# Moving the sample stream's attention beside the gate projections, applying the attention gate at the output projection's input, and spacing the probability split two blocks behind the scores

## The chip, the cores and the metric

The kernel runs on one core of a Trainium2 chip. The metric is the time of one execution in microseconds (us) on the device. The kernel before takes 1334.92 us, the median of three runs between 1334.04 and 1336.14 us.

## The reference

One layer of a streaming encoder for 1024 new frames of one stream (the prompt) and 32 new frames of a running stream (the sample), D = 1024, 16 heads of 64. The two streams differ only in their history: the sample attends to 512 cached frames as well, and its convolution continues a saved state.

```python
h = rmsnorm(x, norm_g)                       # then every projection of h, 1024 columns each:
q = rmsnorm(cols(OFF_Q, ...)) * HEAD_DIM ** -0.5;  k = rmsnorm(cols(OFF_K, ...));  v = cols(OFF_V, ...)
logf = log_sigmoid(cols(OFF_F, N_HEADS) + b_f)
ga, gb, ma, mb = ...                         # gates
u = cols(OFF_UA, ...) * sigmoid(cols(OFF_UB, ...))
s = einsum('bqhd,bkhd->bhqk', q, k) + C[t] - C[s]          # C = cumsum(logf), causal mask
o = softmax(s) @ v
ya = (o * silu(ga)) @ w_pa
yb = (silu(layernorm(causal_dwconv(u))) * silu(gb)) @ w_pb
y = x + (sigmoid(ma) * ya + sigmoid(mb) * yb) @ w_out
```

The results are y, k, v, logf and the convolution's last 30 rows, for both streams.

## The kernel before

**Layout.** Channels lie on the 128 partitions in eight tiles, frames along the free axis: 1056 columns (1024 prompt frames and 32 sample frames), worked in three pieces of 352. A projection of 128 output channels is 24 steps ("beats"): for each of three pieces, eight steps of three matmuls, because every operand is kept as a high and a low part (xh, xl, wh, wl) and three of the four products are formed.

**Stages in order of time**, with the stretches of the profiled execution: the first projections, the convolution's input and v (to about 184 us); k and q (184 to 496), where line 969 makes the high halves `qh` and line 970 the low halves `ql`, which go to DRAM; the projection of the gate `ga` (496 to 579); the prompt's attention (579 to 1036); the remainder of the gate projections and the loads for the next stage (1036 to 1064); the three output projections pa, pb and out (to the end).

**What sets the order.** In the first stages TensorE, VectorE and ScalarE run in the order in which the code issues their instructions; the other queues are ordered by the compiler's scheduler. `beat()` (line 204) counts steps, lets `prep` and `late` jobs out when their step has come, and hands out convolution taps (line 379 on VectorE) from the list `taps` at a rate per step. `begin()` (line 226) plans the next pair of weights: load at steps 5 and 15, sum of squares on ScalarE, a total by a small matmul, then the split into `wh` and `wl`. In the attention stage SyncE, which issues the DMAs, also runs in written order, and an instruction that waits holds up those behind it.

**The prompt's attention.** There are eight groups of two heads. Each group has 16 blocks ("units"): eight query blocks of 128 frames for each of two heads, with 128 to 1024 keys. A unit goes through `scores` (TensorE, into one of two PSUM tiles `psS`), `top` (VectorE, the row maximum), `soft` (ScalarE, the exponential P, which frees `psS`), `factor` (VectorE, the reciprocal of the sum), `high` (ScalarE, P times the factor as 16-bit values in PH), `low` (the rest of P into PH's second half: VectorE for the first head, two GpSimd instructions for the second), and `turn` (SyncE, a transposing DMA from PH to PT). In round k the loop issues unit k's scores and then `factor` and `high` of unit k-1, so `high` of one unit stands on ScalarE ahead of `soft` of the next. Between them `fill_for` issues steps of the projections gb, ma and mb, in proportion to the unit's width plus 320; they keep TensorE busy. P and PH have three buffers each. `values(m)` multiplies the turned halves with v for two query blocks, LAG = 5 rounds behind, and `gated(m)` scales the result (ScalarE) and multiplies it by the gate's slice (GpSimd, line 1282), which `load_gate` (line 1258) fetched; the product goes to DRAM as `s_o`.

**The sample's attention** (`class Sample`, lines 1114 to 1193) handles four heads at a time: loads of cached keys and values and of the cumulative forget sums, scores, maximum, exponential, normalization, five transposes, the product with the values, and one more transpose. Its four parts are put into groups 1, 2, 4 and 6 of the prompt's attention (`SAT`), and take their PSUM tiles from the two pools that the prompt's units use (`psS` and `psT`, two tiles each).

**After the attention.** `a_half(f)` (line 1426) loads a tile of `s_o`, adds the sample's columns, and splits it into `ah` (ScalarE) and `al` (VectorE). Its tiles come from the pool `bg` with five buffers, which the layer norm's output `ln_out` (line 1435) shares. There TensorE alone runs in written order: the last two gate projections, then pa, whose first tile takes its eight input tiles f = 0 to 7 in turn, three pieces of three matmuls each.

Of the kernel before, what the change touches and what calls it, by code (L numbers as in the profile page):

```python
# [18 lines left out]
T = 1024  # L19
TS = 32  # L20
# [17 lines left out]
LAG = 5  # L38
# [4 lines left out]
SAT = (1, 2, 4, 6)  # L43
# [14 lines left out]
def build(tc, xT, xt, wv, wf, ckT, cv, clT, stT, vec, cst, yT, kT, vO, lfO, cpT, csT):  # L58
# [167 lines left out]
    def begin():  # L226
# [21 lines left out]
        if after:  # L248
            jobs += [(5 + 10 * i, after.load) for i in range(after.n)]
# [679 lines left out]
    def qk(g, f):  # L929
# [96 lines left out]
    def gate_steps(g, f, pj):  # L1026
        def ev(c, sl, ps, inv):
            t = t352("t", 3)
            if g == "ga":
                sides["silu"] = nc.scalar.activation(t, ps, AF.Silu, scale=inv)  # L1030
            else:
                nc.scalar.mul(t, ps, inv)
            stored(lambda: nc.sync.dma_start(s_g[g][f, :, sl], t))

        return steps((g, f), X, XL, pj, ev)
# [37 lines left out]
    tables_again("silu")  # L1073
# [3 lines left out]
    order.close()  # L1077
    pcv.close()
# [35 lines left out]
    class Sample:  # L1114


        def __init__(self, g):
            self.g = g

        def load(self):  # L1120
            g = self.g
            self.kc = kc = ap.tile([128, 2, PAST], F32, name="kc", tag="kc", bufs=1)
            nc.sync.dma_start(kc, ckT[2 * g:2 * g + 2].rearrange("a p n -> p a n"))
            self.vc = vc = ap.tile([128, 4, 256], F32, name="vc", tag="vc", bufs=1)
            nc.sync.dma_start(vc, cv[:, :, 256 * g:256 * g + 256])
            self.pf = pf = ap.tile([128, SKEYS], F32, name="pf", tag="pf", bufs=1)
            for j in range(4):
                nc.sync.dma_start(pf[32 * j:32 * j + 32, :], s_cs[4 * g + j:4 * g + j + 1, :].broadcast_to([32, SKEYS]))

        def scores(self):  # L1130
            g, kc, pf = self.g, self.kc, self.pf
            ps = psS.tile([128, 2, 512], F32, name="psS", tag="S")
            for j in range(4):
                rows = slice(64 * (j % 2), 64 * (j % 2) + 64)
                q = qs_t[rows, 2 * g + j // 2, :]
                nc.tensor.matmul(ps[32 * j:32 * j + 32, 0, :], q, kc[rows, j // 2, :], start=True, stop=True)
                nc.tensor.matmul(ps[32 * j:32 * j + 32, 1, :TS], q, ks_t[rows, 2 * g + j // 2, :],
                                 start=True, stop=True)
            self.ps = ps

        def top(self):
            g, ps, pf = self.g, self.ps, self.pf
            nc.vector.scalar_tensor_tensor(pf[:, :PAST], ps[:, 0, :], cq[:, g:g + 1], pf[:, :PAST],
                                           op0=ALU.add, op1=ALU.subtract)
            nc.vector.scalar_tensor_tensor(pf[:, PAST:], ps[:, 1, :TS], cq[:, g:g + 1], pf[:, PAST:],
                                           op0=ALU.add, op1=ALU.subtract)
            nc.vector.tensor_add(pf[:, PAST:], pf[:, PAST:], smask)
            self.nm = nm = ap.tile([128, 3], F32, name="nmr", tag="nmr", bufs=2)
            nc.vector.tensor_reduce(nm[:, 0:1], pf, axis=AX.X, op=ALU.max, negate=True)

        def soft(self):
            nc.scalar.activation(self.pf, self.pf, AF.Exp, bias=self.nm[:, 0:1], accum_out=self.nm[:, 1:2])

        def norm(self):
            nm, pf = self.nm, self.pf
            nc.vector.reciprocal(nm[:, 2:3], nm[:, 1:2])
            nc.vector.tensor_scalar(pf, pf, nm[:, 2:3], None, op0=ALU.mult)

        def turn(self):
            pf = self.pf  # L1160
            self.pts = pts = ap.tile([128, 7, 128], F32, name="pts", tag="kc", bufs=1)
            g = self.g
            nc.gpsimd.memset(pts[:, 4:7, :], 0.0)
            self.vn = pts[:, 5:7, :].rearrange("p a n -> p (a n)")
            nc.sync.dma_start(pts[:TS, 5:7, :], s_vs[:, 256 * g:256 * g + 256].rearrange("p (a n) -> p a n", a=2))
            pt = psT.tile([128, 512], F32, name="ptr2", tag="T")
            for b in range(4):
                nc.tensor.transpose(pt[:, 128 * b:128 * b + 128], pf[:, 128 * b:128 * b + 128], ident)
            nc.scalar.copy(pts[:, 0:4, :], pt.rearrange("p (b q) -> p b q", b=4))
            pt = psT.tile([128, 512], F32, name="ptr2", tag="T")  # L1170
            nc.tensor.transpose(pt[:TS, :128], pf[:, PAST:], ident)
            nc.scalar.copy(pts[:TS, 4, :], pt[:TS, :128])

        def values(self):

            vc, vn, pts = self.vc, self.vn, self.pts
            po = psT.tile([128, 512], F32, name="po", tag="T")
            for b in range(5):
                for j in range(4):
                    hs = slice(64 * j, 64 * j + 64)  # L1180
                    nc.tensor.matmul(po[32 * j:32 * j + 32, :64], pts[:, b, 32 * j:32 * j + 32],
                                     vc[:, b, hs] if b < 4 else vn[:, hs], start=(b == 0), stop=(b == 4))
            self.oq = ap.tile([128, 64], F32, name="oq", tag="oq", bufs=1)
            nc.scalar.copy(self.oq, po[:, :64])

        def finish(self):

            g = self.g
            pt = psT.tile([128, 512], F32, name="ptr2", tag="T")
            nc.tensor.transpose(pt[:64, :128], self.oq, ident)  # L1190
            p4 = pt[:64, :128].rearrange("d (a b n) -> d a b n", a=2, b=2)
            nc.scalar.copy(os_t[0:64, 2 * g:2 * g + 2, :], p4[:, :, 0, :])
            nc.vector.tensor_copy(os_t[64:128, 2 * g:2 * g + 2, :], p4[:, :, 1, :])

    class Unit:
# [22 lines left out]
        def soft(self):  # L1218
            self.P = ap.tile([128, T], F32, name="P", tag="P", bufs=3)
            with tc.issue_after(sides["tables"].ins):  # L1220
                nc.scalar.activation(self.P[:, :self.w], self.ps[:, :self.w], AF.Exp, bias=self.nm[:, 0:1],  # L1221
                                     accum_out=self.nm[:, 1:2])
# [29 lines left out]
    class Pair2:  # L1252
# [539 lines left out]
```

## Time and profile before

The times are microseconds of one profiled execution, whose span is 1332.6 and whose own time was 1334.77, against the median of 1334.92 of the runs that were timed. "Busy" is the time in which an engine worked; matmuls are pipelined, so their durations overlap, and a busy TensorE is not at its peak. The clock is the share of full speed that TensorE was granted.

| stretch | length | TensorE busy | VectorE busy | ScalarE busy | GpSimd busy | clock | DMA share |
|---|---|---|---|---|---|---|---|
| 0 to 496 (up to k and q) | 496.00 | 481.05 | 418.92 | 314.07 | 263.98 | 0.99 | 0.39 |
| 496 to 579 (gate ga) | 83.00 | 83.00 | 76.46 | 32.96 | 14.35 | 1.00 | 0.39 |
| 579 to 1036 (attention) | 457.00 | 396.35 | 334.85 | 276.35 | 218.09 | 0.95 | 0.88 |
| 1036 to 1070 (last gates, loads) | 34.00 | 34.00 | 17.04 | 23.14 | 11.49 | 1.00 | 0.96 |
| 1070 to the end | 263.00 | 259.36 | 155.28 | 88.26 | 138.52 | 1.00 | 0.51 |

A row of such a view has the stretch, its length, and for each engine the busy time and the number of instructions in brackets, then the granted clock, the mean busy share of the 16 DMA engines (it can come out above 1) and what they moved in GB/s. In a row of waits stand the instruction that waited, what released it, the sum of the waits, their number and the longest.

### The profile page before, as it was taken

To read this page: it belongs to the slowest core of one execution; us is meant where nothing else is said; L and a number is where in the kernel's file an instruction comes from. 1 tells how busy PE (TensorE), PEld (TensorE's weight loads), DVE (VectorE), ACT (ScalarE), POOL (GpSimd) and SP (SyncE) were. 2 spreads that over 40 slices of the span, in tenths; PEclk is the share of its full clock that TensorE was granted. 3 is DMA by queue.
4 is the path that set the end of the run, shared out by engine and by line. 5 is a ranking of instruction groups with operands and counts; after the bars stand their busy time and mean duration, and the time that the engine had idled before them with its cause. 6 is when DMAs were issued, how large, how long until landed. Compare 5 with 4: busy or idle time off the path is not lost. (4 is left out here: it accounts for less than half of the span.)

```text
span 1332.6 us, 24984 instructions
## 1 busy us (share of the span) xinstructions
PE 1253.8 (94%) x9270; PEld 928.6 (70%) x9270; DVE 1002.5 (75%) x1494; ACT 734.8 (55%) x1376; POOL 646.4 (49%) x622
## 2 busy tenths in 40 slices
PE   8999999998999899998888797988899999999999
PEld 5687876665666566665555564655566699999998
DVE  6799899796988889889787786776566485166674
ACT  5555555766685763456465465756666565133320
POOL 4067674636474632125473454435445286155562
PEclk9999999999999999999899897999999999999999
DMA  6244342424233354349889799989988887444362
GB/s 255 99 123 123 84 121 67 121 77 125 88 112 114 88 167 135 133 120 200 220 173 219 157 211 221 203 174 223 241 193 173 317 270 250 138 130 143 124 214 69
DMA packets 270554, 213.66 MB, mean 160 GB/s; under 512 B 188001, under 2 KB 232929, under 8 KB 270433
## 3 DMA queue, kind: packets, MB, share of 16 engines
q1 hardware_dynamic: 270288, 212.01, 59.3%
q8 instruction: 72, 1.18, 0.4%
q14 instruction: 50, 0.40, 0.1%
q10 hardware_dynamic: 144, 0.07, 0.0%
HBM read 115.04 MB, written 59.22 MB: 131 GB/s over the span
## 5 line engine op out<-in xcount | busy, mean ns | idle before, releaser
L188 PE MATMUL pj<-xh,wh 128*128 128x352 f16 (+2 forms) x1536 | 487.1, 317 | 6.6 <-DVE qn L959 6.3
L188 PE MATMUL pj<-xl,wh 128*128 128x352 f16 (+2 forms) x1536 | 486.2, 317 | 1.4 <-DVE xl L599 1.3
L188 PE MATMUL pj<-xh,wl 128*128 128x352 f16 (+2 forms) x1536 | 486.4, 317 | 0.1
L188 PEld LDWEIGHTS <-wh 128*128 128x128 f16 x3072 | 303.7, 99 | 167.8 <-issue 2.8
L379 DVE SCALAR_TENSOR_TENSOR y<-u,vec_t,y 128x1086 f32<-128x1086 f32 x240 | 356.9, 1488 | 6.2 <-ACT y L376 3.1
L188 PEld LDWEIGHTS <-wl 128*128 128x128 f16 x1536 | 151.8, 99 | 76.8 <-issue 8.1
L1233 ACT ACTIVATE PH<-P,nm 128x256 f16<-128x256 f32 (+7 forms) x128 | 99.0, 773 | 123.0 <-issue 43.0
L146 DVE SCALAR_TENSOR_TENSOR wl<-raw,sc,wh 128x384 f16<-128x384 f32 x188 | 137.6, 752 | 22.3 <-ACT wh L143 20.9
L1239 POOL TENSOR_SCALAR P<-P,nm 128x128 f32<-128x128 f32 (+3 forms) x64 | 56.6, 885 | 162.5 <-ACT PH L1233 162.1
L1221 ACT ACTIVATE P<-psS,nm 128x256 f32<-128x256 f32 (+7 forms) x128 | 93.6, 731 | 42.0 <-DVE nm L1216 39.4
L1210 PE MATMUL psS<-KB,QB 128*128 128x512 f16 (+2 forms) x192 | 64.2, 334 | 43.3 <-ACT P L1221 43.1
L1216 DVE TENSOR_REDUCE nm<-psS 128x1 f32<-128x256 f32 (+7 forms) x128 | 95.9, 749 | 8.3 <-PE psS L1212 8.2
L180 POOL TENSOR_TENSOR wl<-raw,wh 128x384 fp32r<-128x384 f32 (+1 forms) x51 | 62.8, 1260 | 71.6 <-ACT wh L177 42.9
L1240 POOL TENSOR_TENSOR PH<-P,PH 128x128 f16<-128x128 f32 (+3 forms) x64 | 85.1, 1330 | 5.1
L1242 DVE SCALAR_TENSOR_TENSOR PH<-P,nm,PH 128x128 f16<-128x128 f32 (+3 forms) x64 | 69.0, 1078 | 22.0 <-ACT PH L1233 20.2
L944 POOL TENSOR_TENSOR sql<-sqf,sqh 128x352 fp32r<-128x352 f32 x48 | 54.1, 1127 | 62.8 <-ACT sqh L941 62.6
L970 POOL TENSOR_TENSOR ql<-qn,qh 128x352 f16<-128x352 f32 (+1 forms) x48 | 60.5, 1270 | 20.0 <-ACT qh L969 19.5
L813 PE MATMUL pjv<-vwh,xh 128*128 128x260 f16 x256 | 70.2, 274 | 0.0
L813 PE MATMUL pjv<-vwl,xh 128*128 128x260 f16 x256 | 70.0, 274 | 0.0
L813 PE MATMUL pjv<-vwh,xl 128*128 128x260 f16 x256 | 70.0, 273 | 0.0
L1226 DVE RECIPROCAL nm<-nm 128x1 f32<-128x1 f32 x128 | 20.3, 158 | 61.5 <-ACT P L1221 61.0
L119 ACT ACTIVATE junk<-raw 128x1024 bf16<-128x1024 f32 x62 | 65.0, 1048 | 0.0
(299 smaller groups left out, 2679.9 us busy)
## 6 DMA issues: line engine op xcount, KB each, us to landing
raw<-wf SPq DMA_DIRECT2D x92, 512.0 KB
kT<-kun SPq DMA_DIRECT2D x8, 528.0 KB
s_ga<-t SPq DMA_DIRECT2D x24, 176.0 KB
s_gb<-t SPq DMA_DIRECT2D x24, 176.0 KB
s_ma<-t SPq DMA_DIRECT2D x24, 176.0 KB
s_mb<-t SPq DMA_DIRECT2D x24, 176.0 KB
sma<-s_ma SPq DMA_DIRECT2D x24, 176.0 KB
y<-s_y SPq DMA_DIRECT2D x8, 528.0 KB
```

Of the source, the lines that this page charges most:

```text
L119: nc.scalar.activation(junk[:, :raw.shape[1] * raw.shape[2]], raw.rearrange("p a b -> p (a b)"), AF.Square, accum_out=self.tops[:, i:i + 1])
L146: nc.vector.scalar_tensor_tensor(wl[:, ks, :], raw[:, ks, :], self.s[:, i:i + 1], wh[:, ks, :], op0=ALU.mult, op1=ALU.subtract)
L180: nc.gpsimd.tensor_sub(wl[:, k0:k1, :], raw[:, k0:k1, :], f32(wh[:, k0:k1, :]))
L188: nc.tensor.matmul(ps, a[:, kt, :], b(kt, sl), start=(first and n == 0), stop=(last and n == N - 1))
L379: t = nc.vector.scalar_tensor_tensor(y, u[:, i:i + CW], w, y, op0=ALU.mult, op1=ALU.add)
L813: nc.tensor.matmul(ps[:, :VC], a, b, start=(n == 0), stop=(n == 23))
L1210: nc.tensor.matmul(ps[:, ksl], QB[:, qsl], KB[:, ksl], start=True, stop=False)
L1216: nc.vector.tensor_reduce(self.nm[:, 0:1], self.ps[:, :self.w], axis=AX.X, op=ALU.max, negate=True)
L1221: nc.scalar.activation(self.P[:, :self.w], self.ps[:, :self.w], AF.Exp, bias=self.nm[:, 0:1], accum_out=self.nm[:, 1:2])
L1233: nc.scalar.mul(self.H[:, :n, 0, :], self.P3, self.nm[:, 2:3])
L1240: nc.gpsimd.tensor_sub(self.H[:, :n, 1, :], self.P3, self.H[:, :n, 0, :])
L1242: nc.vector.scalar_tensor_tensor(self.H[:, :n, 1, :], self.P3, f, self.H[:, :n, 0, :], op0=ALU.mult, op1=ALU.subtract)
```

## The change

1. **The sample's attention moves** out of the prompt's attention into the projection of `ga`: its four parts become `late` jobs, 47 steps apart. Its PSUM tiles now come from the pools `st` (two buffers) and `tr` (one buffer) of that stage, and its SBUF tiles from a pool of its own.
2. **The gate is applied later.** The projection of `ga` stores its raw values; `load_gate` and the GpSimd product in `gated` are gone; `a_half` loads the gate's tile, applies Silu on ScalarE and multiplies on VectorE, for prompt and sample columns together.
3. **`high`, `low` and `turn` run two units behind** the scores; `factor` stays one behind and moves after `top`. P and PH get four buffers, the store tile `ot` two, and LAG becomes 6.
4. **Weights are loaded later**: at steps 16 and 26 of the pair before, not 5 and 15.
5. **`qh` and `ql`** get four buffers in place of two.

```diff
-LAG = 5
+LAG = 6
...
-            jobs += [(5 + 10 * i, after.load) for i in range(after.n)]
+            jobs += [(16 + 10 * i, after.load) for i in range(after.n)]
...
-            qh = tp.tile([128, CH], F16, name="qh", tag="qh")
-            ql = tp.tile([128, CH], F16, name="ql", tag="ql")
+            qh = tp.tile([128, CH], F16, name="qh", tag="qh", bufs=4)
+            ql = tp.tile([128, CH], F16, name="ql", tag="ql", bufs=4)
...
             t = t352("t", 3)
-            if g == "ga":
-                sides["silu"] = nc.scalar.activation(t, ps, AF.Silu, scale=inv)
-            else:
-                nc.scalar.mul(t, ps, inv)
+            nc.scalar.mul(t, ps, inv)
...
     u_proj(7, pj)
+    tables_again()
...
+    sp = pool("sp", 1, stack=psm, side="right")
...
-            ps = psS.tile([128, 2, 512], F32, name="psS", tag="S")
+            ps = [st.tile([128, 512], F32, name="psR", tag="st") for _ in range(2)]
...
-            pt = psT.tile([128, 512], F32, name="ptr2", tag="T")
+            pt = tr.tile([128, 512], F32, name="ptr2", tag="tr")
...
-            po = psT.tile([128, 512], F32, name="po", tag="T")
+            po = st.tile([128, 512], F32, name="po", tag="st")
...
+    for g in range(4):
+        smp = Sample(g)
+        for k, fn in ((1, smp.load), (15, smp.scores), (16, smp.top), (22, smp.soft), (26, smp.norm), (33, smp.turn),
+                      (39, smp.values), (44, smp.finish)):
+            later(47 * g + k, fn)
...
-    tables_again("silu")
...
-            self.P = ap.tile([128, T], F32, name="P", tag="P", bufs=3)
+            self.P = ap.tile([128, T], F32, name="P", tag="P", bufs=4)
...
-            self.H = ap.tile([128, 8, 2, 128], F16, name="PH", tag="PH", bufs=3)
+            self.H = ap.tile([128, 8, 2, 128], F16, name="PH", tag="PH", bufs=4)
...
-                self.ot = ap.tile([128, 512], F32, name="ot", tag="ot", bufs=1)
+                self.ot = ap.tile([128, 512], F32, name="ot", tag="ot", bufs=2)
...
-            nc.gpsimd.tensor_mul(ot[:, sl], ot[:, sl], self.gate[:, sl])
...
-            if m % 2 == 0:
-                at(k - 2, lambda p=p, m=m: p.load_gate(m // 2))
...
-        if g in SAT:
-            smp = Sample(SAT.index(g))
...
+    for k in range(len(units) + 2):
+        u, v, w = [unit(k - n) for n in range(3)]
         if u:
             u.scores()
-        if last:
-            last.factor()
-            last.high()
+        if w:
+            w.high()
         fill_for(rate * (u.w + WB) / 2 if u else 2.0)
         if u:
             u.top()
             u.soft()
-        if last:
-            last.low()
+        if w:
+            w.low()
+        if v:
+            v.factor()
...
-        if last:
-            last.turn()
+        if w:
+            w.turn()
...
-    gs = sg2.tile([128, 8, TS], F32, name="gs", bufs=1)
-    nc.sync.dma_start(gs, s_g["ga"][:, :, T:].rearrange("f p n -> p f n"))
-    nc.vector.tensor_mul(os_t, os_t, gs)
-
     def a_half(f):
-        a = big("a3")
+        a, g = big("a3"), big("g3")
         nc.sync.dma_start(a[:, :T], s_o[f, :, :T])
+        nc.sync.dma_start(g, s_g["ga"][f])
         nc.vector.tensor_copy(a[:, T:], os_t[:, f, :])
+        nc.scalar.activation(g, g, AF.Silu)
+        nc.vector.tensor_mul(a, a, g)
         nc.scalar.copy(ah[:, f, :], a)
         nc.vector.tensor_sub(al[:, f, :], a, f32(ah[:, f, :]))
```

**Where instructions now stand.** First, ScalarE in the middle of a group of the attention. In the kernel before, the exponential of a unit (L1221, `P`) is followed by that same unit's high half (L1233, `PH`; 128x5x128 is 640 keys); `t` is the copy of a gate projection's piece, `junk` the sum of squares of a weight, `ot` the scaled output.

```order
L1221 ACTIVATE P,nm<-psS,nm 128x640
L1233 ACTIVATE PH<-P,nm 128x5x128
L1032 ACTIVATE t<-pj,sc 128x352
L1221 ACTIVATE P,nm<-psS,nm 128x640
L1281 ACTIVATE ot<-po,vsc 128x256
L1233 ACTIVATE PH<-P,nm 128x5x128
```

In the changed kernel the exponential (now L1226) is followed by the high half (now L1238) of the unit before:

```order
L1226 ACTIVATE P,nm<-psS,nm 128x640
L1238 ACTIVATE PH<-P,nm 128x4x128
L1028 ACTIVATE t<-pj,sc 128x352
L1226 ACTIVATE P,nm<-psS,nm 128x640
L1238 ACTIVATE PH<-P,nm 128x5x128
L118 ACTIVATE junk,tops<-raw 128x1024
L1226 ACTIVATE P,nm<-psS,nm 128x768
```

A high half no longer needs the sum that the exponential directly ahead of it has just made.

Second, TensorE in the projection of `ga`, where the first part of the sample's attention transposes its probabilities `pf` into `ptr`. Before, only the steps of the projection (L188) stand in this stage, and the small totals of the weights. Now five transposes stand between two steps:

```order
L187 LDWEIGHTS wh
L187 MATMUL pj<-xl,wh 128x352
L1117 MATMUL ptr_6530<-ident,pf 128x128 x4
L1120 MATMUL ptr_6536<-ident,pf 32x128
L187 LDWEIGHTS wh
L187 MATMUL pj<-xh,wh 128x352
```

The fifth writes another tile than the first four (ptr_6536, ptr_6530), and both come from the pool `tr`, which has one buffer.

Third, ScalarE between the attention and pa. Before, the eight high halves `ah` of the input (L1430) stand ahead of the last of the copies `t` of the gate projections' pieces; the last rows of that stretch are:

```order
L1032 ACTIVATE t<-pj,sc 128x352
L1430 CAST ah<-a_13138 128x1056
L1430 CAST ah<-a_13143 128x1056
L1430 CAST ah<-a_13148 128x1056
L1032 ACTIVATE t<-pj,sc 128x352
L177 CAST wh<-raw 128x1024
```

In the changed kernel the last `t` stands ahead of the third `ah` (L1425); each `ah` needs the Silu of its gate tile `g` (L1423), and six tiles are still to come:

```order
L1028 ACTIVATE t<-pj,sc 128x352
L1423 ACTIVATE g_13073<-g_13073 128x1056
L176 CAST wh<-raw 128x1024
L1028 ACTIVATE t<-pj,sc 128x352
L1425 CAST ah<-a_13072 128x1056
L1423 ACTIVATE g_13082<-g_13082 128x1056
L1425 CAST ah<-a_13081 128x1056
L1423 ACTIVATE g_13091<-g_13091 128x1056
L1425 CAST ah<-a_13090 128x1056
L1423 ACTIVATE g_13100<-g_13100 128x1056
L1425 CAST ah<-a_13099 128x1056
```

Between the last product with v and pa, TensorE's order has 180 matmuls of the gate projections, and had 192.

More of the change, by code (lines that the diff above doesn't have):

```diff
@@ L42 @@
 PBO = (0, 4, 1, 5, 2, 6, 3, 7)
-SAT = (1, 2, 4, 6)
 SKEYS = PAST + TS
@@ L1077, in build @@
     order.close()
+    psm.close()
     pcv.close()
@@ L1112, in fill @@
             next(flow, None)
[L1114 to L1131, printed above, removed]
-            ps = psS.tile([128, 2, 512], F32, name="psS", tag="S")
[L1133 to L1165, printed above, removed]
-            pt = psT.tile([128, 512], F32, name="ptr2", tag="T")
[L1167 to L1176, printed above, removed]
-            po = psT.tile([128, 512], F32, name="po", tag="T")
[L1178 to L1193, printed above, removed]
@@ L1256, in __init__ @@
             self.hd, self.pt = hd, {}
-        def load_gate(self, c):
-            self.gate = ap.tile([128, 512], F32, name="ga", tag="ga", bufs=1)
-            nc.sync.dma_start(self.gate, s_g["ga"][self.hd.g, :, 512 * c:512 * c + 512])
         def values(self, m):
@@ L1352, in build, with unit @@
             k = t + 4 * m + 3 + LAG
-            if m % 2 == 0:
-                at(k - 2, lambda p=p, m=m: p.load_gate(m // 2))
             at(k, lambda p=p, m=m: p.values(m))
             at(k + 1, lambda p=p, m=m: p.gated(m))
-        if g in SAT:
-            smp = Sample(SAT.index(g))
-            for k, fn in ((1, smp.load), (5, smp.scores), (6, smp.top), (7, smp.soft), (8, smp.norm), (10, smp.turn),
-                          (12, smp.values), (14, smp.finish)):
-                at(t + k, fn)
-    for k in range(len(units) + 1):
-        u = units[k] if k < len(units) else None
-        last = units[k - 1] if 0 < k <= len(units) else None
+    def unit(k):
+        return units[k] if 0 <= k < len(units) else None
+    for k in range(len(units) + 2):
+        u, v, w = [unit(k - n) for n in range(3)]
         if u:
             u.scores()
-        if last:
-            last.factor()
-            last.high()
+        if w:
+            w.high()
         fill_for(rate * (u.w + WB) / 2 if u else 2.0)
```

66 lines of the change are left out of this document (added).

## The prediction

> **What bounds the kernel now.** I read the page's table of engines first, then the stretches, then the waits inside the attention, and at the end single rows.
>
> ```profile
> PE 1253.8 (94%) x9270; PEld 928.6 (70%) x9270; DVE 1002.5 (75%) x1494; ACT 734.8 (55%) x1376; POOL 646.4 (49%) x622
> ```
>
> TensorE (PE) is busy for 94% of the span. A gain must come from the other 6%, or from time in which it is busy at a reduced clock. The stretches show where both lie:
>
> ```profile
> 496.00:579.00 83.00, 83.00 (x563) 54.44 (x561) 76.46 (x83) 32.96 (x49) 14.35 (x12) 1.00 0.39 127
> 579.00:1036.00 457.00, 396.35 (x3283) 256.24 (x3281) 334.85 (x651) 276.35 (x572) 218.09 (x211) 0.95 0.88 197
> 1036.00:1070.00 34.00, 34.00 (x227) 24.34 (x226) 17.04 (x21) 23.14 (x31) 11.49 (x10) 1.00 0.96 351
> ```
>
> In the projection of `ga` (496 to 579) TensorE is never idle. In the attention it is idle for 457 - 396.35 = 60.7 us, and a mean clock of 0.95 over 457 us takes away another 0.05 x 457 = 23 us of work. So up to 84 us could go there. The groups of the attention, cut at the first scores of 128 keys of each:
>
> ```profile
> 579.00:625.00 46.00, 40.36 (x291) 25.02 (x289) 40.86 (x71) 29.67 (x61) 21.73 (x20) 1.00 0.78 175
> 625.00:690.00 65.00, 53.59 (x479) 35.52 (x477) 49.19 (x91) 36.56 (x75) 33.11 (x30) 0.95 0.87 202
> 690.00:749.00 59.00, 48.48 (x391) 30.31 (x391) 47.28 (x83) 32.77 (x70) 31.42 (x28) 0.91 0.91 211
> 749.00:805.00 56.00, 47.48 (x374) 30.29 (x373) 47.56 (x81) 31.65 (x63) 26.59 (x23) 0.94 0.78 177
> 805.00:866.00 61.00, 53.48 (x432) 34.02 (x431) 40.92 (x82) 38.74 (x83) 27.16 (x30) 0.89 0.95 216
> 866.00:921.00 55.00, 49.27 (x400) 32.02 (x400) 41.04 (x98) 35.76 (x77) 25.89 (x28) 0.97 0.93 202
> 921.00:977.00 56.00, 48.78 (x441) 31.61 (x437) 34.16 (x77) 34.38 (x73) 22.59 (x25) 0.97 1.02 221
> 977.00:1020.00 43.00, 40.73 (x348) 27.19 (x345) 26.14 (x63) 30.77 (x64) 21.99 (x24) 1.00 0.80 166
> ```
>
> Every group has the same prompt blocks and nearly the same gate steps, yet they take 43 to 65 us; 16 us follow the last. The last group, with no taps on VectorE (DVE, third busy column), no sample and no loads for a next group, shows TensorE's own pace: 43 us at full clock. Who makes TensorE wait in the others:
>
> ```profile
> PE psS L1210 <- ACT P L1221: 43.1, 35, 3.8
> PE psS L1136 <- ACT P L1221: 7.6, 3, 3.0
> PE po L1270 <- DMA PT<-PH: 5.7, 5, 1.8
> ```
>
> ```profile
> ACT PH L1233 <- issue: 43.0, 20, 3.6
> ACT PH L1233 <- DMA PT<-PH: 42.2, 19, 5.3
> ACT P L1221 <- DVE nm L1216: 39.4, 39, 2.5
> ACT PH L1233 <- DVE nm L1227: 15.5, 18, 3.3
> ```
>
> TensorE waits 43.1 us for a score tile that ScalarE (ACT) has yet to empty with its exponential, and 7.6 us more for one that the sample's scores took. ScalarE is late because it stands at `high`: 42.2 us until a transposing DMA has read a PH buffer, 15.5 us until VectorE has made the factor from the exponential just ahead, and 43.0 us for which the profile names no releaser. It also waits 39.4 us for the row maximum, since VectorE is late itself.
>
> **The change part by part.** The sum is made against this execution's 1334.77 us (a span of 1332.6 and 2.2 around it); the median of the runs is 1334.92, the same within 0.01%.
>
> **Attention: -60 us (bounds -16 and -78).** With `high` two units behind, the wait for the factor (15.5 us) has a whole round for cover. PH has four buffers, so a transposing DMA has about one round more, some 3 us of a 3.6 us round (457/128), and most of the 42.2 us stands where narrow units follow wide ones, at group starts:
>
> ```profile
> L1233 ACT ACTIVATE PH<-P,nm 128x256 f16<-128x256 f32 x16 | 8.1, 507 | 34.6 <-DMA PT<-PH 29.4 <-DVE nm L1216 2.4 <-DVE nm L1227 2.3
> ```
>
> 29.4 of it stand before the units of 256 keys. The sample's loads, score tiles and VectorE work leave, as do the gate's loads and GpSimd's product. What is late next is VectorE in the groups with taps: 49.19, 47.28 and 47.56 us busy in groups 1 to 3. The sample's work there, by the instructions on its tile `pf`:
>
> ```profile
> 579.00:1036.00 457.00, 3.19 (x20) 2.32 (x20) 10.77 (x20) 3.32 (x8) 0.95 0.88 197
> ```
>
> Its VectorE time is 10.77 us, 2.7 for each of the four parts. VectorE then needs 44.5 to 47.6 us in these three groups, and I give them 50. In groups 4 to 6 TensorE at full clock needs 53.48 - 0.11 x 61 = 46.8, then 47.6 and 47.1, less 2.9 for a sample part in two of them; I give 48. Group 0: 44 in place of 46. Sum: 44 + 3 x 50 + 3 x 48 + 43 + 16 = 397 against 457. DMA allows it on average: group 3 moves 177 x 56 = 9.9 MB, less 0.5 of gate, in 48 us is 196 GB/s, below the 221 of group 6. The tail's last wait (the 1.8 us above, for the last transposed block) gets 1.8 us of gate steps more ahead of it (12 matmuls): -1.
>
> **Projection of `ga`: +16 us (bounds +12 and +22).** TensorE was full, so what it gets is added.
>
> ```profile
> 829.98 1.08 PE L1136 MATMUL psS<-kc,qs_t 64*32 64x512 f32 x8
> ...
> 844.89 0.60 PE L1168 MATMUL ptr<-ident,pf 128*128 128x128 f32 x4
> ...
> 853.97 0.65 PE L1181 MATMUL po<-vc,pts 128*32 128x64 f32 x32
> ```
>
> A part costs 1.1 us of scores (eight small products among them), 0.6 + 0.3 of transposes, 0.8 of products with v and about 0.1 for the last transpose: 2.9 us, four times 11.6. The fifth transpose now waits until ScalarE has emptied the tile of the first four, since `tr` has one buffer:
>
> ```profile
> L1169 ACT COPY pts<-ptr x4: 569/574/575, 670.2 to 956.3; 128x512 f32<-128x512 f32 x4
> ```
>
> That is 0.6 us if ScalarE is free, and 1.7 behind an instruction as long as the casts quoted further down (1.07); I take 1.1, four times 4.4. VectorE gets 4 x 2.7 = 11 on 76.46, 87.3 of about 99: covered, but if it falls behind by more than the seven steps between `norm` and `turn`, TensorE waits there (the upper bound). The loads, 1 MB and four short ones a part at 351 GB/s, need 3 us of the 6 that lie between load and scores, with DMA at 0.39: nothing. The Silu and its table load leave ScalarE, which was 40% busy: nothing.
>
> **k and q: -6 us (bounds 0 and -10).** `qh` and `ql` had two buffers, and ScalarE stood until DMAs had read them:
>
> ```profile
> ACT qh L969 <- DMA s_k<-qh: 14.4, 6, 3.4
> ```
>
> ```profile
> PE pj L188 <- DVE qn L959: 6.3, 4, 2.1
> PE pst L925 <- POOL sql L944: 2.2, 2, 1.8
> ```
>
> TensorE's waits of 6.3 and 2.2 us are behind that. One of them also costs clock:
>
> ```profile
> 304.00:312.00 8.00, 5.88 (x40) 3.90 (x39) 0.58 (x1) 5.19 (x10) 2.51 (x5) 1.00 0.59 132
> 312.00:320.00 8.00, 7.96 (x42) 4.74 (x42) 4.61 (x6) 4.53 (x9) 6.30 (x7) 0.79 0.56 172
> ```
>
> After 2.1 idle us the next 8 run at 0.79, a loss of 1.7. Together 10; not every wait need be DMA's, so 6. The weights' later loads still land 25 steps, 11 us, ahead of their first use; a load takes 3 to 6 us: nothing, and if that cover fails TensorE waits for `wl`.
>
> **Before pa: +17 us (bounds +5 and +20).** Here the change adds a wait. A tile f needs two loads, then Silu, product, `ah`, `al`, and takes two of five buffers. The order puts `ah` of tile 2 behind the last gate piece, and a cast of weights stands ahead of both; that cast waits for the last gate step already:
>
> ```profile
> 1064.42 1.05 ACT L177 CAST wh<-raw 128x1024 fp32r<-128x1024 f32 x1 [1.08 <-PE pj L188]
> ```
>
> The durations, the load's first row, and pa's pace:
>
> ```profile
> L1430 ACT CAST ah<-a x8: 1061/1072/1074, 1045.0 to 1061.8; 128x1056 fp32r<-128x1056 f32 x8
> L1431 DVE TENSOR_TENSOR al<-a,ah x8: 1251/1258/1445, 1046.1 to 1062.9; 128x1056 fp32r<-128x1056 f32 x8
> ```
>
> ```profile
> 1038.77 0.58 SPq L1428 DMA_DIRECT2D a<-s_o  x1
> ...
> 1045.02 1.07 ACT L1430 CAST ah<-a 128x1056 fp32r<-128x1056 f32 x1 [0.59 <-DMA a<-s_o]
> ```
>
> ```profile
> 1100.00:1125.00 25.00, 25.00 (x160) 25.00 (x159) 17.59 (x16) 16.02 (x20) 19.16 (x10) 1.00 0.87 284
> ```
>
> A load landed 6.3 us after its issue with two weights ahead of it (1.5 us each at 351 GB/s), so 3.3 alone. Count from the last gate step, when pa would begin: cast 1.05, gate piece 0.55, `ah` 1.07, `al` 1.26, with handoffs 4.3: tile 2 is there. Only then is a buffer free for the gate of tile 4: 3.3 + 1.07 (Silu, taken as the cast of that shape) + 1.26 (product, taken as `al`) + 1.07 + 1.26 = 8.0, so 12.3. Tile 3 at 8.0 in the same way gives tile 5 at 16.3; tile 7's gate loads behind that, and ScalarE's order puts its Silu ahead of `ah` of tile 6: 23.0 and 24.4. pa does a tile in nine matmuls of 25/160 us, 1.4: it ends tile 7 at 25.8, not at 8 x 1.4 = 11.3. That is a stall of 14.5 in four pieces of 1.5 to 6 us. With the clock as after 312 I add 2.5.
>
> [...] The rows at 304 to 320 show a drop after 2.1 us of idling, so I go by them.
>
> The lower bound is ScalarE's queue alone, eleven instructions of 1.07 behind the cast and the piece, +5; the upper has both loads slower. The layer norm's output moves behind these loads, and has cover until pb, some 90 us later.
>
> **Sum:** -60 - 1 + 16 - 6 + 17 = -34: 1334.77 - 34 = 1301 us.
>
> **The rivals.** *VectorE sets the groups with taps.* For: it is 84% busy over groups 1 to 3 already (144.0 of 180), and the same passes are to fit into less time. Against: part of its idle time is the wait for ScalarE that goes. If groups 1 to 3 take 54 and 4 to 6 take 49, attention is 46 + 162 + 147 + 43 + 16 = 414, -43, and the total 1318.
>
> *TensorE sets all groups.* For: the last group. If 1 to 6 take 46 each and group 0 takes 44, attention is 379, -78, and the total 1283.
>
> *The transposes set the pace, and two units of distance only move the wait (slower).* For: groups 3 and 5 have no sample and still take 56 and 55; DMA stands at 0.93 to 1.02 in groups 5 and 6. PH's four buffers then fill as three did, and ScalarE waits as long, a round later. Groups 1 to 6 stay at 56: 46 + 336 + 43 + 16 = 441, only -16; k and q, where DMA is not full, give nothing in the worst case; with +16 and, on a full DMA queue, +20 before pa, 1354. It decides from a mean of groups 1 to 6 above 54.5 us, where the attention's gain falls below the 26 that the other terms cost. Against: the last group has 0.80 of DMA and the old order, and hardly waits; 9.6 MB leave the stage (4.2 of gate, 5.4 of sample).
>
> **How the numbers follow.** Forecast 0.48; VectorE 0.22; TensorE 0.15; transposes 0.10; the rest, between the last and the others, 0.05. A measurement of this kernel tells about 0.2% (2.7 us) from no change. Faster 0.86, the same 0.03, slower 0.11. The range reaches from a little below TensorE's case to above VectorE's: 1274 to 1328.
>
> **What would show it.** Right: the attention near 400 us with psS waits below 15; clock near 0.98 there; the `ga` stretch near 99 with no wait on `kc` loads; waits of TensorE for `al` in the first tile of pa, some 14 us. Wrong: group times that stay at 55; TensorE waiting for VectorE's normalization in the `ga` stretch; no gap before or in pa's first tile.

## The result, and the profile after

The changed kernel takes 1317.53 us (median of four runs, 1315.72 to 1320.59) against 1335.16 (four runs, 1334.04 to 1336.14) for the kernel before beside it: a ratio of 0.9871, interval 0.9848 to 0.9893, or 17.6 us less. The forecast was 1301, a gain of 34 us; half of it came. The profiled execution is the slowest of the four: 1320.59 us, with a span of 1318.8, so the terms below add up to 13.7 us, not to 17.6. Of the executions of all the runs below one, of e10, took 3251 us; it is left out of that run's ratio.

The page's table of engines, then the stretches that answer to those shown before (start:end, length, busy time and instructions of PE, PEld, DVE, ACT and POOL, clock, DMA share, GB/s):

```profile
PE 1255.5 (95%) x9270; PEld 935.9 (71%) x9270; DVE 1006.2 (76%) x1501; ACT 738.2 (56%) x1382; POOL 626.5 (48%) x590
```

```profile
486.00:581.00 95.00, 91.39 (x790) 58.72 (x789) 81.04 (x104) 37.94 (x70) 14.04 (x16) 1.00 0.49 159
```

```profile
581.00:1006.00 425.00, 383.94 (x3048) 254.46 (x3046) 323.72 (x627) 264.19 (x545) 190.10 (x176) 0.95 0.88 190
```

```profile
1006.00:1033.00 27.00, 27.00 (x182) 17.92 (x181) 6.51 (x8) 15.24 (x23) 5.28 (x6) 1.00 0.91 344
1033.00:1060.00 27.00, 17.46 (x66) 13.91 (x65) 18.26 (x17) 14.68 (x15) 3.70 (x3) 0.67 0.78 257
```

TensorE works as long as before (1255.5 to 1253.8 us); what went is idle time, 78.8 to 63.3 us. The attention lost a third of its 60.7 idle us, not all, and its clock is 0.95 as before. Behind it stands a new stretch in which TensorE is idle for 9.5 of 27 us at a clock of 0.67.

To compare terms I cut both traces at the same events: the first store of `s_ga` (501.5 before, 491.3 after), the first scores of the attention (578.8, 581.0), the last product with v (1035.4, 1005.5), and the end of the span.

| term | forecast | measured |
|---|---|---|
| up to ga (k and q) | -6 | -10.2 |
| projection of ga | +16 | +12.4 |
| attention | -60 | -32.0 |
| from the last product with v to the end | -1 + 17 | 297.2 to 313.3: +16.1 |
| sum | -34 | -13.7 (spans: -13.8) |

Three terms came out within 5 us of the forecast. The attention alone is 28 us off. Its groups, cut at their first scores of 128 keys (by these events two of the prediction's cuts for the kernel before, at 690 and 866, stood 3.7 us late and 2.2 early; the busy times of single groups shift by up to 4 us with that, their sums hardly):

| group | 0 | 1 | 2 | 3 | 4 | 5 | 6 | 7 | behind the last scores | all |
|---|---|---|---|---|---|---|---|---|---|---|
| before | 46.0 | 61.5 | 62.6 | 56.6 | 62.7 | 51.8 | 55.8 | 43.3 | 16.2 | 456.5 |
| forecast | 44 | 50 | 50 | 50 | 48 | 48 | 48 | 43 | 16 | 397 |
| after | 42.0 | 56.3 | 51.6 | 53.1 | 55.1 | 50.4 | 48.2 | 46.9 | 21.0 | 424.5 |

Groups 1 to 3 are 11 us over the forecast, 4 to 6 are 10 over, group 7 and what follows 9 over. The table of waits for this stage shows who is waited for now (instruction, releaser: sum, number, longest):

```profile
ACT P L1226 <- DVE nm L1221: 62.2, 39, 6.0
DVE nm L1221 <- PE psS L1217: 49.3, 29, 8.9
ACT P L1226 <- DVE nm L1231: 34.5, 27, 3.9
...
PE psS L1215 <- ACT P L1226: 19.6, 13, 4.8
PE po L1271 <- DMA PT<-PH: 18.3, 9, 3.4
...
ACT PH L1238 <- DMA PT<-PH: 11.6, 7, 2.9
```

The waits that the change was to remove did shrink: PE for `psS` from 43.1 to 19.6, ACT for a PH buffer from 42.2 to 11.6 (its waits there with no releaser named from 43.0 to 8.2), and the factor is hardly waited for (2.3 in place of 15.5). Two others grew: ScalarE's exponential waits 62.2 + 34.5 us for VectorE (39.4 before), and TensorE 18.3 us for transposed blocks (5.7 before). The second row of ScalarE names the reciprocal at L1231, which an exponential does not need. The timeline of group 2 shows what it is (VectorE, then ScalarE):

```profile
730.56 1.34 DVE L378 SCALAR_TENSOR_TENSOR y<-u,vec_t,y 128x1086 f32<-128x1086 f32 x1
731.82 1.22 DVE L1221 TENSOR_REDUCE nm<-psS 128x1 f32<-128x1024 f32 x1
732.96 0.15 DVE L1231 RECIPROCAL nm<-nm 128x1 f32<-128x1 f32 x1
```

```profile
733.13 1.11 ACT L1226 ACTIVATE P<-psS,nm 128x1024 f32<-128x1024 f32 x1 [1.66 <-DVE nm L1231]
```

The maximum ends at 731.82 + 1.22 = 733.04 and the exponential starts at 733.13; the reciprocal merely began in between. Both rows are therefore waits for `top`, which stood behind a tap.

### The profile page after: what moved, and what is told of

The parts are those of the page before. It is cut to its first block, busy times and chain, and to the rows that moved or that the text cites. A ratio compares the mean times of both kernels' runs of the same rounds, so it can differ in the third digit from the quotient of the medians.

```text
span 1318.8 us, 24980 instructions
## 1 busy us (share of the span) xinstructions
PE 1255.5 (95%) x9270; PEld 935.9 (71%) x9270; DVE 1006.2 (76%) x1501; ACT 738.2 (56%) x1382; POOL 626.5 (48%) x590
## 5 line engine op out<-in xcount | busy, mean ns | idle before, releaser
L145 DVE SCALAR_TENSOR_TENSOR wl<-raw,sc,wh 128x384 f16<-128x384 f32 x188 | 144.2, 790 | 27.6 <-ACT wh L142 26.2
L1244 POOL TENSOR_SCALAR P<-P,nm 128x128 f32<-128x128 f32 (+3 forms) x64 | 63.1, 986 | 207.7 <-ACT PH L1238 207.7
L1226 ACT ACTIVATE P<-psS,nm 128x256 f32<-128x256 f32 (+7 forms) x128 | 94.3, 737 | 101.4 <-DVE nm L1221 62.2
L1221 DVE TENSOR_REDUCE nm<-psS 128x1 f32<-128x256 f32 (+7 forms) x128 | 96.2, 752 | 49.6 <-PE psS L1217 49.3
L1238 ACT ACTIVATE PH<-P,nm 128x256 f16<-128x256 f32 (+7 forms) x128 | 98.5, 770 | 29.0 <-DMA PT<-PH 11.6
L1028 ACT ACTIVATE t<-pj,sc 128x352 f32<-128x352 f32 x96 | 52.6, 548 | 71.3 <-PE pj L187 66.5
L943 POOL TENSOR_TENSOR sql<-sqf,sqh 128x352 fp32r<-128x352 f32 x48 | 56.6, 1182 | 64.7 <-ACT sqh L940 64.7
L1271 PE MATMUL po<-PT,Vh 128*64 128x256 f16 (+1 forms) x640 | 69.5, 305 | 18.4 <-DMA PT<-PH 18.3
L1215 PE MATMUL psS<-KB,QB 128*128 128x512 f16 (+2 forms) x192 | 62.9, 328 | 22.7 <-ACT P L1226 19.6
L1247 DVE SCALAR_TENSOR_TENSOR PH<-P,nm,PH 128x128 f16<-128x128 f32 (+3 forms) x64 | 62.9, 983 | 20.9 <-ACT PH L1238 20.9
L187 PE MATMUL pj<-ah,wh 128*128 128x352 f32 x192 | 65.1, 339 | 5.2 <-ACT ah L1425 5.2
```

Of the source, the lines that this page charges most:

```text
L145: nc.vector.scalar_tensor_tensor(wl[:, ks, :], raw[:, ks, :], self.s[:, i:i + 1], wh[:, ks, :], op0=ALU.mult, op1=ALU.subtract)
L187: nc.tensor.matmul(ps, a[:, kt, :], b(kt, sl), start=(first and n == 0), stop=(last and n == N - 1))
L1221: nc.vector.tensor_reduce(self.nm[:, 0:1], self.ps[:, :self.w], axis=AX.X, op=ALU.max, negate=True)
L1238: nc.scalar.mul(self.H[:, :n, 0, :], self.P3, self.nm[:, 2:3])
L1244: nc.gpsimd.tensor_scalar(self.P3, self.P3, f, 1.0, op0=ALU.mult, op1=ALU.mult)
L1271: nc.tensor.matmul(po[64 * e:64 * e + 64, 128 * ii.start:256], v[:, j, 64 * e:64 * e + 64], pt[:, ii, e, j, x, :], start=(j == 0 and n == ...
```

## The experiments

Times are medians; the kernel before took 1334.4 to 1335.7 in the same sessions.

**e1: taps out.** Taps of the convolution's last tiles are left out: the trace has 196 in place of 240, so 44, where the expectation counted 48.

```diff
-            t = nc.vector.scalar_tensor_tensor(y, u[:, i:i + CW], w, y, op0=ALU.mult, op1=ALU.add)
+            if sides.get("no_taps") and i < KC - 1:
+                return 1.0
+            t = nc.vector.scalar_tensor_tensor(y, u[:, i:i + CW], w, y, op0=ALU.mult, op1=ALU.add)
...
-    sides["queue"] = True
+    sides["queue"] = sides["no_taps"] = True
```

> The changed kernel with 48 of the 240 convolution taps left out, those that VectorE works during the attention (72.7 us of its time there); all else stands. VectorE theory (its tops come late because taps and weight splits stand ahead of them): groups 0 to 3, now 42.0, 56.3, 51.6 and 53.1 us, fall to 42, 48, 48 and 48, the waits of ScalarE's exponential for VectorE (62.2 + 34.5 us) fall below 50, and the total falls by 12 to 18 us from 1317.5. Transpose theory (DMA sets the groups): groups 1 to 3 stay above 51 and the total stays within 4 us of 1317.5.

Measured: 1300.63 us, ratio 0.9744 (0.9727 to 0.976), 16.9 below the changed kernel. The groups take 38.9, 49.4, 51.8, 47.9, 51.9, 50.0, 48.3, 47.0 and 20.9 us, together 406.1: 18.4 less, in groups 0, 1, 3 and 4. VectorE's theory holds in the sum; group 2 did not move, and ScalarE still waits 67.5 us for VectorE, more than the 50 expected. Its waits show what stands behind VectorE:

```profile
ACT P L1228 <- DVE nm L1223: 47.6, 26, 5.1
ACT PH L1240 <- DMA PT<-PH: 23.9, 13, 3.6
ACT P L1228 <- DVE nm L1233: 19.9, 17, 3.9
PE po L1273 <- DMA PT<-PH: 19.2, 10, 3.8
PE psS L1217 <- ACT P L1228: 10.7, 9, 2.9
```

TensorE's wait for `psS` halves (19.6 to 10.7), and ScalarE's wait for PH doubles (11.6 to 23.9). In group 2 the DMA share is 1.03:

```profile
668.00:720.00 52.00, 46.30 (x376) 30.73 (x375) 30.11 (x70) 31.74 (x66) 22.16 (x23) 0.93 1.03 211
```

**e4: taps spread** over groups 0 to 5 by a lower rate.

```diff
-R_U, R_V, R_QK, R_G, R_A = 0.21, 0.18, 0.165, 0.23, 0.2
+R_U, R_V, R_QK, R_G, R_A = 0.21, 0.18, 0.165, 0.23, 0.15
```

> The changed kernel with the taps in the attention at 0.15 a step in place of 0.2, so that they reach into groups 4 and 5. VectorE theory: groups 1 to 3 lose a quarter of their taps (4 to 5 us of VectorE each) and get some 3 us shorter each, groups 4 and 5 take 1 to 3 us more, and the total falls by 2 to 7 us. If VectorE does not set these groups, the total stays within 2 us of 1317.5.

Measured: 1321.28 us, ratio 0.9897 (0.9881 to 0.9913): a miss. Groups 1 to 3 fell from 161 to 157 us, less than expected, and groups 4 to 6 rose from 154 to 159. The trace has 9, 8, 9, 9, 10 and 1 taps in groups 0 to 5 (12, 10, 13 and 11 in groups 0 to 3 of the changed kernel), so taps alone do not explain groups 5 and 6, which grew by 4.0 and 4.9 us. The layer norm's statistics, which start when the taps are done, moved too: some 13 us of VectorE's time for them stand in group 6, not in group 5. The lower rate thus moves two things, and what a tap costs in the later groups is not shown.

**e3: products with v one round later.**

```diff
-LAG = 6
+LAG = 7
```

> The changed kernel with the products with v seven rounds behind the scores instead of six. Distance theory (two units of delay for the transposes ate what LAG = 6 gave): TensorE's 18.3 us of waits for PT fall below 8 and the total falls by 6 to 12 us. Transpose theory (the DMA's throughput sets it): ScalarE's wait for a PH buffer grows from 11.6 us by as much as the PT waits fall, and the total stays within 4 us of 1317.5.

Measured: 1311.52 us, ratio 0.9827 (0.9812 to 0.9841), 6.0 less. The waits:

```profile
PE psS L1215 <- ACT P L1226: 32.9, 21, 5.9
ACT PH L1238 <- DMA PT<-PH: 8.5, 8, 2.0
PE po L1271 <- DMA PT<-PH: 2.3, 1, 2.3
```

The 18.3 us for PT were a matter of distance: they go, and the wait for PH does not grow. But 13.3 of these 16.0 us come back as waits for `psS` (19.6 to 32.9), and ScalarE still waits 93.4 us for VectorE. Group 7 takes 42.4 us again.

**e7: one unit behind**, all else of the change kept: the old loop, LAG 5 and three buffers of P and PH.

```diff
-    for k in range(len(units) + 2):
-        u, v, w = [unit(k - n) for n in range(3)]
+    for k in range(len(units) + 1):
+        u = units[k] if k < len(units) else None
+        last = units[k - 1] if 0 < k <= len(units) else None
```

> The changed kernel with high, low and turn one unit behind again (LAG 5, three buffers of P and PH), all other parts of the change in place. The prediction's theory (ScalarE standing at high is most of TensorE's wait): ScalarE's waits at PH come back to 40 to 60 us, TensorE's for psS to 30 us or more, the attention takes 435 to 445 us in place of 424.5 and the total is 1328 to 1338. VectorE theory in its strong form (VectorE alone sets the rounds): the attention stays within 5 us of 424.5.

Measured: 1335.07 us, ratio 0.9998 (0.9985 to 1.0011). The attention takes 442.7 us, ScalarE's named waits at PH come to 51.9 us and TensorE's for `psS` to 48.0, all as expected.

**e8: the gate's part alone**, put on the kernel before (its diff is that of part 2 and of the lines of `a_half`).

> The kernel before with the gate's part of the change alone (raw ga stored, no load and product in the attention, Silu and product in a_half). By the prediction: 13 to 20 us more before pa, 2 to 8 us less in the attention (4.2 MB of loads and 49 us of GpSimd waits leave it), together 1340 to 1352. If the stall before pa needs the other parts too, the total is below 1338.

Measured: 1348.95 us, ratio 1.0097 (1.008 to 1.0114). The attention takes 455.8, only 0.7 less; the time behind its last product is 313.2, 16.0 more. Between them e8, e7 and the changed kernel price the attention's parts, each from one execution and in this order: gate 0.7 us, the sample's move with the later loads of weights 13.1 (455.8 to 442.7), two behind with its buffers and LAG 18.2 (442.7 to 424.5). Neither of the last two was run alone.

**e2, e5, e6: the stall before pa.** In e2 the gate tiles get buffers of their own.

```diff
+    gp = pool("gp", 2, stack=psg2, side="right")
...
-        a, g = big("a3"), big("g3")
+        a, g = big("a3"), gp.tile([128, TT], F32, name="g3", tag="ag")
```

> The changed kernel with two buffers of their own for the gate tiles that the output projection's input loads, so that those tiles no longer take two of five buffers each. Buffer theory (the stall in pa's first tile comes from the sharing): gates turn over in 3.3 + 1.08 + 1.26 = 5.7 us for two tiles and the inputs themselves are all loaded ahead, so TensorE's waits of 5.2 and 4.3 us for ah and al and the half clock behind them nearly go, and the total falls by 12 to 18 us, to 1300 to 1305. Load theory (the DMA queue is late whatever the buffers): the waits stay at 6 us or more and the total falls by less than 6.

Measured: 1323.52 us, ratio 0.9909 (0.9892 to 0.9926), 6 more than the changed kernel, whose interval it just touches. TensorE waits 8.0 us for `ah` and 5.0 for `al`, not 5.2 and 4.3. The timeline of SyncE's queue (rows with x4 are four loads):

```profile
1021.98 4.14 SPq L1481 DMA_DIRECT2D sma<-s_ma  x4
1026.36 0.32 SPq L1029 DMA_DIRECT2D s_mb<-t  x1
1026.77 0.38 SPq L1422 DMA_DIRECT2D g<-s_ga  x1
```

The gate of tile 2 was issued only at 1026.77, behind loads of `sma` and a store. So e5 keeps the buffers and is meant to move the gates up by priority, and e6 has that priority without the buffers:

```diff
     for f in range(8):
-        a_half(f)
+        with tc.high_priority(offset=4000):
+            a_half(f)
```

> The kernel of e2 (gate tiles in two buffers of their own) with the loads, Silu and products of pa's input given priority, so that SyncE's queue has the gates of tiles 2 and 3 behind one store of s_mb and one load of sma, not behind two stores and four loads. Queue theory (in e2 the gate of tile 2 was issued only at 1026.8, behind sma loads that waited for buffers, and that is the stall): TensorE's waits for ah and al fall from 9.5 us to below 5 and the total to 1303 to 1309 us. If neither buffers nor queue are the cause, the waits stay and the total is above 1315.

> The changed kernel with that priority but the five shared buffers as they are. Buffer theory: the gate of tile 2 still needs a buffer that a finished tile gives back, the waits for ah and al stay at 8 us or more and the total stays within 4 us of 1317.5. Queue theory: the waits fall below 6 and the total below 1312.

Measured: e5 1319.65 us, ratio 0.9879 (0.9855 to 0.9903); e6 1317.66, ratio 0.9862 (0.9845 to 0.988). Neither differs from the changed kernel; the time behind the last product is 312.7 and 311.9 us against 313.3, and TensorE still waits 8.9 and 8.3 us. But e5 did not do what it was meant to: its gates of tiles 2 and 3 again stand behind six loads of `sma`.

```profile
1019.06 7.80 SPq L1482 DMA_DIRECT2D sma<-s_ma  x6
1027.55 0.82 SPq L1422 DMA_DIRECT2D g<-s_ga  x2
```

In e6 the gate of tile 2 is issued 15.6 us behind the last product with v, in place of 19.2, and all later ones sooner as well. Tiles 2 to 6 then come ready one step earlier, but tile 7 does not: in the chain that ends last, a load of the layer norm (4.43 us) and one of its passes on VectorE (1.26) stand ahead of its `al`. So buffers alone (e2) and an earlier place alone (e6) do not free the stall; both together were not reached. And e2 changes only the sharing: its gates have two buffers, and the gate of tile f still waits for the product of tile f-2 (that of tile 4 is issued at 1035.70, after 1035.67; that of tile 7 at 1048.10, after 1048.08).

**e9: the gates' loads.** Two gates are loaded and used for all eight tiles, so the rest of e5 stays and 3.24 MB go, and with them the wait for a buffer to load into.

```diff
-        nc.sync.dma_start(g, s_g["ga"][f])
+        if f < 2:
+            nc.sync.dma_start(g, s_g["ga"][f])
```

> The kernel of e5 with the gates of tiles 0 and 1 loaded and used for all eight tiles: six loads of 528 KB are left out (3.24 MB), Silu, products, buffers and the order stay. Volume theory (this stretch had DMA at 0.96 and 345 GB/s already before, so 4.3 MB more is 12.5 us more wherever they queue): six eighths of that go, TensorE's waits before and in pa's first tile fall below 3 us and the total by 8 to 14 us from e5's 1319.65, to 1306 to 1312. Engine theory (Silu, cast, product and rest of eight tiles on ScalarE and VectorE set it): waits of 6 us or more stay and the total is above 1315.

Measured: 1309.27 us, ratio 0.9812 (0.9793 to 0.9831), 10.4 below e5; the time behind the last product falls from 312.7 to 302.2. One wait of 4.13 us for `al` stays, more than expected. VectorE's timeline shows a pass of the layer norm (L1441), itself waiting for its load, ahead of the product (L1431) and of `al` (L1433):

```profile
1040.20 1.28 DVE L1441 TENSOR_TENSOR y<-y,mean 128x1056 f32<-128x1056 f32 x1 [1.68 <-DMA y<-s_y]
1041.40 1.77 DVE L1431 TENSOR_TENSOR a<-a,g 128x1056 f32<-128x1056 f32 x1
1043.10 1.25 DVE L1433 TENSOR_TENSOR al<-a,ah 128x1056 fp32r<-128x1056 f32 x1
```

**e10: the gate back in the attention**, with LAG 7: part 2 of the change is undone (Silu at the projection, `load_gate`, the product on GpSimd, one buffer of `ot`).

> The kernel of e3 (LAG 7) without part 2 of the change: the gate is loaded and multiplied in the attention as in the kernel before (Silu at the projection, product on GpSimd, one ot buffer), so that 4.3 MB less are moved between the attention and pa. Volume theory: the 16.1 us by which the time from the last product with v to the end grew go nearly all, the attention of 419.3 us grows by 0 to 4 (e8 gave 0.7 for this part), and the total is 1295 to 1301, against e3's 1311.5. If the gate's loads and products hold up the attention as much at the new pace, the total stays above 1306.

Measured: 1300.93 us, ratio 0.9744 (0.9725 to 0.9763), faster than both kernels. The time behind the last product is 293.2 us, 18.0 less than in e3, and TensorE is never idle before pa or in its first tile:

```profile
1024.00:1050.00 26.00, 26.00 (x166) 24.41 (x165) 19.36 (x16) 17.37 (x21) 13.11 (x8) 1.00 0.88 317
```

The attention takes 424.5 us, 5.2 more than in e3: the gate's loads and products do cost something at the new pace, though less than before pa.

**e11: ten taps earlier**, on top of e10.

```diff
-R_U, R_V, R_QK, R_G, R_A = 0.21, 0.18, 0.165, 0.23, 0.2
+R_U, R_V, R_QK, R_G, R_A = 0.21, 0.18, 0.18, 0.25, 0.2
```

> The kernel of e10 with more taps a step before the attention (0.18 for 0.165 in k and q, 0.25 for 0.23 in ga), so that 36 in place of 46 are left for it. VectorE theory: e1 gave 18.4 us of attention for 48 taps, 0.38 us each, so ten are worth 3.8; total 2 to 5 us below e10, if VectorE stays ahead of TensorE in k and q (267 of 302 us busy there) and ga. Otherwise TensorE waits for qn or norm there and the total is that of e10 or above.

Measured: 1307.78 us, ratio 0.9804 (0.9781 to 0.9827): the second branch came. The attention falls by 2.2 us to 422.3, but its first scores come at 588.5, not 579.4. In k and q TensorE waits again, 2.0 us for VectorE's `qn` and 1.8 for a total of GpSimd's; its stretch 300 to 400 has only 97.95 us busy, where e10 has 99.86. With 1.2 us more of waits in ga these are some 5 of the 9.1 us; where the rest went was not looked for. VectorE, with 267 of 302 us busy before, had less room there than that let it seem.

## Why the prediction was right and wrong

**The attention: the step that failed.** The forecast's step was "VectorE then needs 44.5 to 47.6 us in these three groups, and I give them 50". The first half was right within 1 us: VectorE is busy for 45.46, 48.37 and 46.02 us there.

```profile
623.00:679.00 56.00, 46.81 (x371) 30.92 (x371) 45.46 (x80) 34.81 (x70) 25.33 (x23) 0.94 0.88 192
679.00:731.00 52.00, 47.30 (x377) 31.13 (x376) 48.37 (x83) 31.54 (x65) 26.98 (x23) 0.93 0.95 203
731.00:784.00 53.00, 47.63 (x376) 31.75 (x374) 46.02 (x79) 30.41 (x64) 24.92 (x20) 0.94 0.88 189
784.00:839.00 55.00, 49.12 (x383) 32.15 (x383) 34.70 (x80) 38.55 (x80) 23.11 (x23) 0.97 0.98 211
...
938.00:985.00 47.00, 43.73 (x353) 29.25 (x351) 26.24 (x61) 29.84 (x64) 17.27 (x19) 0.93 0.78 158
985.00:1006.00 21.00, 17.55 (x162) 13.00 (x161) 10.10 (x17) 6.77 (x11) 9.21 (x8) 0.92 0.64 142
```

But 3 us of slack were too little. VectorE and TensorE wait for each other in turn: with two `psS` tiles a wide unit's `top`, late behind a tap, holds up the next scores, and then VectorE has nothing to do until these have come (49.3 us of waits for `psS` in the table above, 8.2 before). So 4 to 11 us of VectorE's time in a group are lost, and TensorE's longest waits for `psS` stand where narrow units follow (4.01, 2.29 and 4.80 us at the second scores of groups 2, 3 and 4). e1 measures it: without the taps the whole stage takes 18.4 us less, and groups 1 to 3 take 49.7 on average, which is what I had given them with the taps in. This is the rival "VectorE sets the groups with taps": 54 us forecast for groups 1 to 3, 53.7 measured; 49 for groups 4 to 6, 51.2 measured. But it gave the whole attention 414 us, and 424.5 were measured; its total of 1318 was met with luck, since k, q and ga gave 8 us more than forecast while groups 4 to 6 took 7 more than it said and group 7 and the tail 9 more. Of the forecast's own signs the attention near 400, a `psS` wait below 15 and a clock near 0.98 did not come (424.5, 19.6, 0.95).

Groups 4 to 6 failed in the same way: I gave them TensorE's time at full clock and 3 us on top (45.2 on average by the prediction's own terms, 48 given). Group 6 came so (48.2), group 5 took 2.4 us more and group 4 7.1. Group 4 starts with the wait of 4.80 us. Directly ahead of the `top` in question VectorE has no tap but the two passes of the convolution's sums that follow the last tap (L344 and L351, 2.5 us); e1 keeps these, leaves the taps out, and waits 1.66 us there, so about 3 of the 4.80 are the taps'.

Group 7 and the tail were forecast by rows of the old order, where nothing waited. LAG 6 makes up for the later `turn` in rounds, but the rounds are shorter: the wait for PT, which the forecast had as nearly gone, is 3.3 us in group 7 and 3.4 in the tail, and the clock is 0.93 and 0.92 there. e3 shows that it is the distance: with one round more group 7 is back at 42.4. The tail is not: it takes 22.2 us in e3, 21.0 with LAG 6 and 15.2 with LAG 5 (e7), so a longer distance is itself paid behind the last scores, which the forecast had at nothing.

**What was right in the attention.** That `high` two units behind frees ScalarE: e7 prices it, with its buffers and LAG, at 18.2 us, and with it undone the waits at PH come back (30.4 for the DMA, 21.5 for the factor, 38.4 without a name). The sample's leaving, with the weights' later loads, gave 13.1. The transposes as the pace, the slower rival, did not come: groups 1 to 6 have a mean of 52.4, below the 54.5 at which it decides. e1 suggests that they are next behind VectorE.

**Before pa: right size and right order, with luck in the load.** The time grew by 16.1 us, forecast 16. pa starts 1.8 us sooner behind the last product and then its first tile takes 29.1 us, not 11.7. Counted from pa's first matmul at 1032.40, `al` of tiles 2 to 7 is ready after 4.6, 8.7, 12.2, 16.7, 24.2 and 25.4 us; the forecast, which counts from nearly the same moment, had 4.3, 8.0, 12.3, 16.3, 23.0 and 24.4. The chain that ended last shows the buffers given back in turn, as forecast: the gate of tile 5 is issued when the product of tile 3 ends, that of tile 7 when the product of tile 5 ends.

```profile
1038.69 5.59 DMA g<-s_ga
1044.37 1.09 ACT g L1423
1045.49 1.27 DVE a L1424
1046.77 4.87 DMA g<-s_ga
1051.73 1.09 ACT g L1423
1052.84 1.26 DVE a L1424
1054.17 1.26 DVE y L1434
1055.43 1.18 DVE al L1426
1056.65 7.49 PE pj L187 x28
```

But a turn of 8.0 us was met by two errors that cancel. The loads take 5.59 and 4.87 us, not the 3.3 that I took for a load alone, in a stretch that had 0.96 of DMA and 351 GB/s already before (the row quoted in the prediction); and a gate's buffer is free after the product, not after `ah` and `al`, which saves 2.3. One pass of the layer norm (L1434), which the sum had at nothing, stands ahead of the `al` of tile 6.

That the gates' loads are the cause is shown: with six of eight left out pa's first tile takes 18.4 us (e9, 28.1 in e5), with none there 11.7 (e10). Whether it is their 4.3 MB (12.3 us at 351 GB/s) or the turns of the buffers is not separated, since e9 and e10 take both away; a run with more buffers for the same loads is missing.

The split between waits and clock looks wrong, 9.5 us of waits (14.5 forecast) and some 8 of low clock (2.5 forecast), but the slow matmuls of the earlier tiles ran in time in which pa would have waited. Tile 7 was ready after 25.4 us, and nine matmuls take 1.44 at full clock, as those of the second tile do (1033.99 to 1035.43): by that estimate the low clock added 29.1 - 26.8 = 2.3 us.

**k and q: right, larger.** All of TensorE's waits went, and the clock loss behind them; ScalarE no longer waits for DMAs at `qh` (14.4 and 7.9 us before):

```profile
184.00:486.00 302.00, 301.86 (x2028) 201.52 (x2026) 266.81 (x320) 212.27 (x380) 172.80 (x166) 1.00 0.39 111
```

The forecast had 10 as all there was to win and took 6; the time came to the 10 within its accuracy. No run undoes part 5 alone, so that the buffers did it is read from these waits. **The projection of ga** took 12.4, its lower bound. The wait for the fifth transpose is there, and is TensorE's only wait in this stretch:

```profile
PE ptr L1120 <- ACT pts L1118: 3.6, 4, 1.6
```

3.6 us stand against 4.4 forecast. The work itself is then 12.4 - 3.6 = 8.8 us, or 2.2 a part and not 2.9, presumably since the durations that I added overlap: of the second part's scores, eight products start at 512.41 and take 1.08 us, and the next eight start at 513.29 already.

## What to carry to other kernels

When a wait is taken out of a loop of several engines, give the next engine in line its busy time and what it must idle besides, read from a stage of the same kernel; a busy time and some 3 us were 11 us short over three groups here. Before a load is moved to another stage, count its turn there: the wait for a buffer, the way from issue to landing at that stage's DMA share, and the passes that give the buffer back, against the pace of what uses it. Here a turn for two tiles took 8 us, and pa uses two tiles in 2.9. The same 4.3 MB cost 0.7 us in the attention of the kernel before (e8) and 5.2 at the pace of e3 (e10), but 16 to 18 before pa; with LAG 7 the kernel is 0.8% faster with them left in the attention (e10 against e3). A distance in rounds shrinks in time when the rounds get shorter.

## What the runs showed of the hardware

TensorE never idled for more than 2.21 us in pa's first tile, and it ran at half clock for 16 us (1044 to 1060), and below full clock just before and after:

```profile
1040.00:1044.00 4.00, 2.53 (x11) 1.72 (x11) 2.95 (x4) 1.83 (x2) 0.00 (x0) 0.78 1.00 379
1044.00:1048.00 4.00, 2.86 (x10) 2.07 (x8) 2.18 (x4) 2.31 (x3) 0.00 (x0) 0.50 0.92 292
1048.00:1052.00 4.00, 3.28 (x9) 2.37 (x9) 2.31 (x2) 1.11 (x2) 0.00 (x0) 0.50 0.88 268
1052.00:1056.00 4.00, 0.96 (x2) 0.50 (x2) 3.09 (x3) 3.41 (x4) 0.00 (x0) 0.50 0.61 193
1056.00:1060.00 4.00, 3.35 (x11) 3.35 (x12) 4.00 (x4) 1.56 (x2) 0.00 (x0) 0.50 0.80 268
1060.00:1064.00 4.00, 4.00 (x19) 4.00 (x19) 4.00 (x6) 3.52 (x5) 1.07 (x1) 0.66 0.46 164
```

Of two matmuls of 352 columns, each behind a wait, the one at 1037.02 took 0.43 us and the one at 1043.39 took 0.66.

VectorE's taps of one shape have a median of 1.343 us and a mean of 1.552 in the attention, up to 2.620 (group 2 has some of 1.95 to 2.28). What stretches them was not tried.
